# A changed order for the last attention heads, the head norms and the out projection of a two-layer trunk

## The chip, the cores and the metric

The kernel runs on one core of one Trainium2 chip, as one program. The metric is device time in microseconds (us) of an execution, as a median of runs; lower is better. Before the change it is 1693.77 us, the median of 3 runs (1693.08 to 1694.43).

## What is computed

The reference is one step of a two-layer diffusion trunk over 640 tokens of width 1024: 512 latent tokens (tiles 0 to 3 of 128) and 128 context tokens (tile 4). Layer 0 mixes tokens by differential attention, layer 1 by neighbourhood attention on a grid; each is followed by an out projection, a gated residual with layer norm, and a squared-ReLU MLP.

```python
def block(qb):                                   # differential attention, 8 heads
    logits = jnp.einsum('bqhmd,bkhmd->bhmqk', qb, k, preferred_element_type=jnp.float32) * scale
    p = jax.nn.softmax(logits, -1)
    a = p[:, :, 0] - lam * p[:, :, 1]
    return jnp.einsum('bhqk,bkhe->bqhe', a, v).astype(v.dtype)
o = map_query_blocks(block, q)
o = rms_norm(o, subln) * (1.0 - DIFF_LAMBDA_INIT)          # per head: the "head norms"
...
y = attention(x * (1 + scale) + shift) @ w_o                # out projection
x = layer_norm(ALPHA * x + gate * y, ln_g, ln_b)
x = layer_norm(ALPHA * x + gate2 * sq_relu_mlp(x * (1 + scale2) + shift2), ...)
```

Latent tokens read their own keys and the context tokens of a cache; context tokens read context tokens only. All matrix products keep float32 accuracy: every operand is split into a high and a low part (`hhi`/`hlo` for activations, `wh`/`wl` for weights, `aT` high and low for attention weights), and three matmuls (lines 120, 121, 122) make one product.

## The kernel before, in words

TensorE (PE) does the matmuls in an order that is written out by hand: `ORDER0` and `ORDER1` are lists of tokens, and `run` calls the function behind each token in turn. What a token issues to the other engines, VectorE (DVE), ScalarE (ACT), GpSimd (POOL) and the queue of SP, is put in order by the framework's scheduler, and each engine then runs its list strictly in that order.

The tokens of the first layer that matter here, h for a head (0 to 7), b for a tile of queries, t for a tile of tokens, hf for a half of the 1024 output columns:

- `q{h}{t}`, `v{h}{t}`: 24 matmuls of the query/key or the value projection. `r{h}{t}`: PE transposes of rotated queries and keys (line 521); ACT and DVE then write the high and low parts `q` and `K` (lines 523 to 527).
- `S{h}{b}`: scores (lines 461, 462), row maxima on DVE (`mx`, L576), exp on ACT (`E`, L578), difference of the two maps on DVE (L586). `T{h}{b}`: transposes of `E` (L597), then ACT and DVE write `aT` (lines 127, 128). `P{h}`: attention weights times values. `c{h}`, `C{h}`: the same for context queries.
- `Q{h}`: sums of squares of a head's output by matmuls with `mean` (L632); for heads 3, 5, 6, 7 the function `rstd0` (L633 to L652: small DVE steps and one square root on ACT) follows. `D5` (`rn_rows`): a PE transpose, a DVE copy to `rnr` (L659) and a DMA from SP to the DRAM rows `rnd` (L660).
- `N{h}`, the norm of a head. For heads 0 to 5: POOL issues a DMA that broadcasts the row of `rnd` into `X[:, 7, :]` (L727), and one DVE instruction (L728) scales the head's output. There is one such buffer, so the broadcast of one head waits for the scaling of the head before it. For heads 6 and 7 the factor goes through PE (`dg`, L674) and two DVE instructions (L675).
- `m{g}`, `M{g}`: units of the modulation vectors; they also release raw weight buffers `rw`, of which there are three. `X` (`swap`): finishes the modulation, casts heads 0 to 5 to `hhi` on ACT and subtracts on DVE to `hlo`, loads the gates and the residual. These write over the input `h` of the query projections, so they come after the last `q` unit.
- `o{hf}{t}`: the out projection over k tiles 0 to 5 (18 matmuls). `j{hf}{t}`: its k tiles 6 and 7. `g{t}`: gate and residual; `h{t}`: layer norm and transposes; `f{x}`: first units of the MLP.

PSUM has eight banks: four in the pool `M` (512 columns each), and two tiles of two banks for the scores (`S`). A part `o` takes its space in one of three ways. In `before` the way follows from its number x in the list (hf, t): x below `early` (4 in layer 0, 5 in layer 1): a bank of `M`, and `add_gated` (L1084, L1086) at once takes the sum to SBUF, so that `j` starts a fresh bank; the next two: a bank of `M`, held until `g`; the rest: half of a score tile, held until `g`. In layer 0 this gives o00 to o03 early, o04 and o10 held in `M`, o11 to o14 held in a score tile. The second gate tile, which the context tile t = 4 needs, has its broadcast DMA (L735, `gate<-gates`) in a buffer that is free only after the scores S73.

Layer 1 has the same tail with its own letters (`t`, `B`, `Y`, `Z` beside them): `X` there casts heads 0 to 5 and `Y` head 6.

Of the kernel before, what the change touches and what calls it, by code (L numbers as in the profile page):

```python
# [36 lines left out]
EARLY0, EARLY1, PARTS = 4, 5, (10, 9)  # L37
# [4 lines left out]
    e0 e4 A e2 v10 e1 m8 v13 b e3 r00 r04 q10 r02 q14 r01 q12 r03 m9 M8 S00 r10 v11 S01 r11 v12 c0 r14 v14 M9  # L42
    T00 S02 q21 q20 q30 r12 m10 T01 S03 r13 q23 m11 T02 S10 T03 r20 q31 C0 c1 M10 P0 m12 T10 S11 M11 r21 M12
    q22 S12 m13 q24 r22 T11 S13 r23 q32 r24 C1 T12 S20 r30 m14 M13 Q0 T13 M14 c2 P1 S21 T20 r31 q33 S22 T21
    q34 r32 Q1 S23 r33 v21 v20 r34 S30 T23 q40 v24 m15 T22 S32 C2 P2 m16 T30 r40 S31 q42 M16 q41 c3 r42 q43
    q44 T31 S33 r43 v22 r41 v23 M15 C3 r44 Q2 T32 q50 T33 S40 m17 P3 m18 S41 M18 q52 c4 Q3 T40 q51 v33 D3 r51
    r50 q53 M17 S42 v31 r52 q54 T41 S43 r54 r53 v30 S50 T43 v34 T42 v32 S51 q70 q61 C4 P4 c5 m19 T50 q60 m20
    M19 S52 r60 M20 q62 m21 r61 T52 q63 T51 S53 r62 M21 q64 r63 m22 r64 T53 C5 S60 M22 Q4 P5 S61 q71 m23 N2 c6
    Q5 M23 r70 q72 r71 T60 S62 D5 N1 T61 q73 N0 r72 q74 S63 N3 C6 T62 N4 N5 X r73 r74 o00 S70 T63 o02 c7 P6
    o03 T70 S71 Q6 o01 T71 D6 S72 o04 o10 T72 S73 C7 N6 o11 T73 o12 P7 o13 Q7 D7 o14 N7 j00 j10 j01 j11 g0 j12  # L50
    g1 j02 j13 h0 g2 j03 j04 h1 j14 g3 g4 h2 f0 f2 h3 f3 h4 f1
# [1392 lines left out]
```

## Time and profile before

| what | us |
|---|---|
| median of 3 runs | 1693.77 |
| the profiled execution | 1694.21 |
| its span in the trace | 1692.4 |
| PE busy | 1611.3 (95%) |
| DVE busy | 1098.9 (65%) |
| ACT busy | 669.0 (40%) |
| POOL busy | 316.4 (19%) |

The span leaves 1.81 us of the execution outside the trace. PE is the engine that is nearly always busy; 1692.4 - 1611.3 = 81 us of its span are idle. The mean granted clock of TensorE is 0.983 of full speed. Times in the trace are counted from the start of the span: layer 0's tail (from head 5 to the first MLP units) lies at about 300 to 435 us, layer 1's at about 1130 to 1275 us. In a row of the timeline the number in brackets is idle time of that engine before the instruction, with the instruction that ended it.

### The profile page before, as it was taken

To read this page: it belongs to the slowest core of one execution; us is meant where nothing else is said; L and a number is where in the kernel's file an instruction comes from. 1 tells how busy PE (TensorE), PEld (TensorE's weight loads), DVE (VectorE), ACT (ScalarE), POOL (GpSimd) and SP (SyncE) were. 2 spreads that over 40 slices of the span, in tenths; PEclk is the share of its full clock that TensorE was granted. 3 is DMA by queue.
4 is the path that set the end of the run, shared out by engine and by line. 5 is a ranking of instruction groups with operands and counts; after the bars stand their busy time and mean duration, and the time that the engine had idled before them with its cause. 6 is when DMAs were issued, how large, how long until landed. Compare 5 with 4: busy or idle time off the path is not lost. (4 is left out here: it accounts for less than half of the span.)

```text
span 1692.4 us, 23972 instructions
## 1 busy us (share of the span) xinstructions
PE 1611.3 (95%) x9074; PEld 1394.7 (82%) x9074; DVE 1098.9 (65%) x2169; ACT 669.0 (40%) x1366; POOL 316.4 (19%) x260
## 2 busy tenths in 40 slices
...
GB/s 336 130 136 91 102 116 151 103 129 52 124 113 137 199 149 187 162 172 103 75 75 161 126 127 119 148 140 165 14 112 113 63 99 75 76 98 51 100 51 63
DMA packets 61367, 200.62 MB, mean 119 GB/s; under 512 B 7765, under 2 KB 14403, under 8 KB 60227
## 3 DMA queue, kind: packets, MB, share of 16 engines
...
q14 instruction: 45, 0.36, 0.1%
...
## 5 line engine op out<-in xcount | busy, mean ns | idle before, releaser
L195 ACT CAST wh<-rw 128x1024 fp32r<-128x1024 f32 x192 | 200.2, 1053 | 380.1 <-PE M L122 287.9
L197 DVE TENSOR_TENSOR wl<-rw,wh 128x512 fp32r<-128x512 f32 x278 | 216.1, 811 | 128.7 <-ACT wh L195 128.0
L120 PE MATMUL M<-hhi,wh 128*128 128x512 f32 (+2 forms) x768 | 279.0, 363 | 8.1 <-DVE r L1199 7.9
L122 PE MATMUL M<-hhi,wl 128*128 128x512 f32 (+2 forms) x768 | 277.5, 361 | 1.8 <-DVE wl L197 1.8
L121 PE MATMUL M<-hlo,wh 128*128 128x512 f32 (+2 forms) x768 | 277.1, 361 | 0.0
L120 PE MATMUL M<-wh,uhi 128*128 128x512 f32 x640 | 250.9, 392 | 3.1 <-DVE rc L1199 3.1
L120 PE MATMUL M<-wh,hhi 128*128 128x256 f32 (+1 forms) x752 | 244.6, 325 | 8.7 <-DVE tmp L1143 3.2
L122 PE MATMUL M<-wh,ulo 128*128 128x512 f32 x640 | 249.9, 391 | 1.6 <-DVE ulo L128 1.6
L121 PE MATMUL M<-wl,uhi 128*128 128x512 f32 x640 | 249.9, 390 | 0.0
L197 POOL TENSOR_TENSOR wl<-rw,wh 128x512 fp32r<-128x512 f32 x106 | 181.9, 1726 | 345.0 <-ACT wh L195 344.7
L122 PE MATMUL M<-wh,hlo 128*128 128x256 f32 (+1 forms) x752 | 240.1, 319 | 5.0 <-DVE hlo L128 5.0
L121 PE MATMUL M<-wl,hhi 128*128 128x256 f32 (+1 forms) x752 | 239.5, 319 | 0.0
L120 PEld LDWEIGHTS M<-hhi,wh 128*128 128x128 f32 x768 | 146.1, 190 | 26.1 <-issue 8.2
L122 PEld LDWEIGHTS M<-hhi,wl 128*128 128x128 f32 x768 | 145.9, 190 | 20.8 <-DVE wl L197 3.3
L120 PEld LDWEIGHTS M<-wh,hhi 128*128 128x128 f32 x752 | 145.2, 193 | 20.6 <-DVE tmp L1143 3.4
L121 PEld LDWEIGHTS M<-hlo,wh 128*128 128x128 f32 x768 | 146.0, 190 | 17.2
L122 PEld LDWEIGHTS M<-wh,hlo 128*128 128x128 f32 x752 | 144.8, 193 | 17.9 <-DVE hlo L128 9.1
L121 PEld LDWEIGHTS M<-wl,hhi 128*128 128x128 f32 x752 | 145.2, 193 | 8.7
L120 PEld LDWEIGHTS M<-wh,uhi 128*128 128x128 f32 x640 | 120.5, 188 | 28.3 <-issue 3.5
L294 DVE SCALAR_TENSOR_TENSOR jk<-wm,cb 128x1024 bf16<-128x1024 f32 x96 | 141.7, 1476 | 2.9 <-DMA wm<-in_wmodT 1.9
L122 PEld LDWEIGHTS M<-wh,ulo 128*128 128x128 f32 x640 | 120.6, 188 | 27.7 <-DVE ulo L128 2.4
L121 PEld LDWEIGHTS M<-wl,uhi 128*128 128x128 f32 x640 | 120.6, 188 | 25.1 <-DVE wl L197 0.4
(284 smaller groups left out, 2459.9 us busy)
## 6 DMA issues: line engine op xcount, KB each, us to landing
...
```

The costliest lines, as they stand in the source:

```text
L120: te.matmul(out, sh, mh, start=start, stop=False)
L121: te.matmul(out, sh, ml, start=False, stop=False)
L122: te.matmul(out, sl, mh, start=False, stop=stop)
L195: keep(nc.scalar.copy(hi, r))
L197: keep(eng.tensor_tensor(lo[:, k], r[:, k], hi[:, k], ALU.subtract))
L294: op = nc.vector.scalar_tensor_tensor(jk, ws[t], 1.0, cb[:, x, :], ALU.mult, ALU.mult, accum_out=mc[:, t, x : x + 1])
```

## The change

Line numbers of the changed kernel are higher by 2 from line 40 on. Five things change.

1. **The ways of the parts** stand in a table, `PARTS`, with e (early), m (bank of `M`, held) or s (half of a score tile, held) for each. Layer 0 now has o02, o03, o04 and o13 early, o00 and o01 held in `M`, and o10, o11, o12, o14 in a score tile. Layer 1's ways stay as they were.
2. **Layer 0's order after P5.** Before: `S61 q71 m23 N2 c6 Q5 M23 r70 q72 r71 T60 S62 D5 N1 T61 q73 N0 r72 q74 S63 N3 C6 T62 N4 N5 X r73 r74 o00 S70 T63 o02`. After: `q71 S61 r70 q72 r71 N2 q73 Q5 T60 c6 q74 D5 S62 r72 N3 m23 T61 S63 M23 C6 T62 N4 N5 X r73 r74 S70 T63 o02`. So q73 and q74 come ahead, Q5, D5 and m23 later, and S70 T63 stand ahead of the first part.
3. **The parts' order.** Before: `o02 c7 P6 o03 T70 S71 Q6 o01 T71 D6 S72 o04 o10 T72 S73 C7 N6 o11 T73 o12 P7 o13`. After: `o02 c7 P6 o03 T70 S71 Q6 o04 T71 D6 S72 o00 o01 o13 T72 S73 C7 N6 o10 T73 o11 P7 o12`.
4. **Layer 0's end.** g0, g1 and j13 are placed differently among the `j`, and f0 and f2 relative to h2: before `g3 g4 h2 f0 f2`, after `g3 g4 f0 h2 f2`.
5. **Layer 1's order**, one stretch. Before: `P52 c6 q70 B70 S63 t6 T60 S62 q72 X B73 B71 P60 T61 o00 T62 P61`. After: `P52 q70 S63 q72 c6 X B70 t6 T60 S62 B73 B71 P60 o00 T61 T62 P61`.

The tokens N0 to N3 stand earlier in the list (N0 after m20, N1 after r63, N2 after r71, N3 after r72); the scheduler leaves the DVE and POOL instructions of N0 to N3 at the same rows of their engines as before.

```diff
-EARLY0, EARLY1, PARTS = 4, 5, (10, 9)
+PARTS = (
+    "02e 03e 04e 00m 01m 13e 10s 11s 12s 14s",
+    "00e 01e 02e 03e 04e 10m 11m 12s 13s",
+)
...
-    def proj_ops(self, pool, l, late, early, free, ready, tag):
+    def proj_ops(self, pool, l, late, free, ready, tag):
...
-        def slot(x):
-            if x < early + 2:
+        def slot(kind):
+            if kind != "s":
                 return self.M()
...
-        def part(x):
-            hf, t = seq[x]
-            m = slot(x)
-            self.nat(self.h, t, n + hf, m, 0, 512, 0, 6, True, x < early)
-            accs[hf, t] = None if x < early else m
-            if x < early:
+        def part(hf, t, kind):
+            m = slot(kind)
+            self.nat(self.h, t, n + hf, m, 0, 512, 0, 6, True, kind == "e")
+            accs[hf, t] = None if kind == "e" else m
+            if kind == "e":
                 evac = lambda: self.add_gated(late["X"], t, hf, m, late["gate"], True)
...
-        for x, (hf, t) in enumerate(seq):
-            if x < PARTS[l]:
-                op(f"o{hf}{t}", lambda x=x: part(x), "X", *(("Y",) if x >= 2 else ()), *((free,) if x >= early + 2 else ()))
-            op(f"j{hf}{t}", lambda hf=hf, t=t: proj(hf, t), f"o{hf}{t}", *ready)
+        for x, (hf, t, kind) in enumerate(PARTS[l].split()):
+            y = int(hf), int(t), kind
+            op(f"o{hf}{t}", lambda y=y: part(*y), "X", *(("Y",) if x >= 2 else ()), *((free,) if kind == "s" else ()))
+        for hf in range(2):
+            for t in range(NTT):
+                op(f"j{hf}{t}", lambda hf=hf, t=t: proj(hf, t), f"o{hf}{t}", *ready)
```

How the rows move is shown at three places. First PE at the swap of layer 0, in the kernel before, from the last transposes of attention weights ahead of it to the first part (`idf,nt` is r73, `idf,X` is r74, `wh`, `wl` with `hhi`, `hlo` is o00):

```order
L597 MATMUL M_4298<-idf,E_4133 128x128
L320 MATMUL M_4310<-idf,gt_4306 48x128
L521 MATMUL M_4343<-idf,nt_4188 128x128 x3
L521 MATMUL M_4352<-idf,X_549 128x128 x3
L120 MATMUL M_4361<-wh_3396,hhi 128x512
L121 MATMUL M_4361<-wl_3397,hhi 128x512
L122 MATMUL M_4361<-wh_3396,hlo 128x512
```

The same place on PE in the changed kernel (the rows from `K,q` on are S70, those from `idf,E` on are T63, and the last is the first matmul of o02):

```order
L322 MATMUL M_4311<-idf,gt_4307 48x128
L523 MATMUL M_4344<-idf,nt_4076 128x128 x3
L523 MATMUL M_4353<-idf,nt_4188 128x128 x3
L463 MATMUL S_4362<-K_3994,q_546 128x320
L464 MATMUL S_4362<-K_3994,q_546 128x320
L463 MATMUL S_4363<-K_3994,q_546 128x320
...
L599 MATMUL M_4384<-idf,E_4273 128x128 x4
L599 MATMUL M_4391<-idf,E_4273 128x128
L122 MATMUL M_4395<-wh_3396,hhi 128x512
```

The part o00 has left this place; the scores S70 and the transposes T63 follow r74 directly, and the first part is another tile's.

Second, DVE around the copy `rnr` of D5, from which the norms of heads 4 and 5 start. Before:

```order
L576 TENSOR_REDUCE mx_4129<-S_4119 128x1
L576 TENSOR_REDUCE mx_4129<-S_4120 128x1
L659 COPY rnr_4143<-M_4141 10x128
L128 TENSOR_TENSOR aT_4107<-M_4148,aT_4106 128x4x128
L128 TENSOR_TENSOR aT_4107<-M_4155,aT_4106 128x128
```

After (`hlo` is the first of the subtractions of the swap, `wl` a pair of low weight halves):

```order
L130 TENSOR_TENSOR hlo<-X_549,hhi 128x640
L586 RECIPROCAL Z_4124<-Z_4124 128x1
L587 SCALAR_TENSOR_TENSOR c_4125<-Z_4124,zz,neglam 128x1
L578 TENSOR_REDUCE mx_4207<-S_4197 128x1
L588 SCALAR_TENSOR_TENSOR E_4127<-E_4130,c_4125,E_4127 128x128
L578 TENSOR_REDUCE mx_4207<-S_4198 128x1
L199 TENSOR_TENSOR wl_4156<-rw_4147,wh_4155 128x512 x2
L661 COPY rnr_4194<-M_4192 10x128
```

The copy now has one `hlo` and a pair of `wl` ahead of it.

Third, DVE around the scaling of head 5 (N5). Before, where L525 and L527 are the queries and keys of r73 and r74:

```order
L728 SCALAR_TENSOR_TENSOR X_549<-X_549,sub_106 128x640
L128 TENSOR_TENSOR hlo<-X_549,hhi 128x640 x3
L525 SCALAR_TENSOR_TENSOR q_546<-M_4343,q_546 128x2x128
L527 TENSOR_TENSOR K_4051<-M_4343,K_4051 64x128 x2
L525 SCALAR_TENSOR_TENSOR q_546<-M_4352,q_546 128x2x128
L527 TENSOR_TENSOR K_4051<-M_4352,K_4051 64x128 x2
```

After:

```order
L527 SCALAR_TENSOR_TENSOR q_546<-M_4344,q_546 128x2x128
L730 SCALAR_TENSOR_TENSOR X_549<-X_549,sub_106 128x640
L529 TENSOR_TENSOR K_3994<-M_4344,K_3994 64x128 x2
L527 SCALAR_TENSOR_TENSOR q_546<-M_4353,q_546 128x2x128
L130 TENSOR_TENSOR hlo<-X_549,hhi 128x640
L529 TENSOR_TENSOR K_3994<-M_4353,K_3994 64x128 x2
```

The scaling of head 5 and one `hlo` remain ahead of the keys; two `hlo` that followed it have moved to earlier places.

More of the change, by code (lines that the diff above doesn't have):

```diff
@@ L41 @@
 ORDER0 = """
[L42 to L51, printed above, removed]
+    e0 e4 A e2 v10 e1 m8 v13 b e3 r00 r04 q10 r02 q14 r01 q12 r03 m9 M8 S00 r10 v11 S01 r11 v12 c0 r14 v14 M9 T00
@@ L52 @@
+    T51 S53 r62 M21 q64 r63 N1 m22 r64 T53 C5 S60 M22 Q4 P5 q71 S61 r70 q72 r71 N2 q73 Q5 T60 c6 q74 D5 S62 r72 N3
+    m23 T61 S63 M23 C6 T62 N4 N5 X r73 r74 S70 T63 o02 c7 P6 o03 T70 S71 Q6 o04 T71 D6 S72 o00 o01 o13 T72 S73 C7 N6
+    o10 T73 o11 P7 o12 Q7 D7 o14 N7 j00 j10 g0 j01 j11 g1 j12 j02 h0 g2 j03 j04 h1 j13 j14 g3 g4 f0 h2 f2 h3 f3 h4
+    f1
 """
 ORDER1 = """
-    e1 e3 e2 e0 b q03 v04 B00 q00 B03 q01 q02 q12 v11 S00 q10 B01 B02 c0 B10 q11 S01 v13 q13 B12 S02 T00 v12
-    t0 S03 P00 v10 C0 T01 B13 B11 T02 S10 P01 B20 S11 P02 S13 v14 c1 T10 q20 S12 q22 B23 q21 P10 t1 T11 q23 C1
@@ L56 @@
-    T12 P11 S20 B21 q30 S21 q31 c2 T20 P12 B22 q32 S22 q33 S23 t2 B30 q43 v21 P20 T21 v20 S30 q40 C2 B32 T22
-    B31 P21 B33 B40 S31 q41 T30 S33 v23 P22 c3 q42 S32 t3 v24 P30 T31 B42 v22 S40 T32 C3 B41 P31 q50 S41 P32
-    q51 c4 T40 q52 B43 S42 t4 B50 q53 P40 S43 v30 S50 T41 B51 v31 S51 C4 T42 v32 P41 v33 P42 B52 B53 v34 c5
-    T50 q60 P50 S52 q61 S53 t5 q62 B60 T51 q63 B63 S60 B62 B61 C5 T52 P51 q73 S61 q71 P52 c6 q70 B70 S63 t6
-    T60 S62 q72 X B73 B71 P60 T61 o00 T62 P61 C6 S71 P62 o01 Y S70 o02 B72 c7 o03 S72 T70 o04 t7 S73 o10 C7
@@ L61 @@
-    T71 P70 o12 P71 T72 o11 P72 Z o13 j00 j10 j13 g0 j01 j11 j12 g1 j02 h0 g2 j04 j03 g3 h1 j14 g4 h3 h2 f1 f0
-    h4 f3 f2
+    e1 e3 e2 e0 b q03 v04 B00 q00 B03 q01 q02 q12 v11 S00 q10 B01 B02 c0 B10 q11 S01 v13 q13 B12 S02 T00 v12 t0 S03
+    P00 v10 C0 T01 B13 B11 T02 S10 P01 B20 S11 P02 S13 v14 c1 T10 q20 S12 q22 B23 q21 P10 t1 T11 q23 C1 T12 P11 S20
+    B21 q30 S21 q31 c2 T20 P12 B22 q32 S22 q33 S23 t2 B30 q43 v21 P20 T21 v20 S30 q40 C2 B32 T22 B31 P21 B33 B40 S31
+    q41 T30 S33 v23 P22 c3 q42 S32 t3 v24 P30 T31 B42 v22 S40 T32 C3 B41 P31 q50 S41 P32 q51 c4 T40 q52 B43 S42 t4
```

14 lines of the change are left out of this document (11 added, 3 removed).

## Prediction

> **What bounds the kernel now.** I read the page first, then the windows of the two attention tails, then the list of PE's waits, and last the timelines of PE, DVE and POOL at the places that the change touches. The page's first row:
>
> ```profile
> PE 1611.3 (95%) x9074; PEld 1394.7 (82%) x9074; DVE 1098.9 (65%) x2169; ACT 669.0 (40%) x1366; POOL 316.4 (19%) x260
> ```
>
> PE is the bound over the whole run, and the change takes no matmul away and adds none. So it can only move the 1692.4 - 1611.3 = 81 us in which PE stands idle, and time in which it runs at a lower clock. The windows (PE, weight loads, DVE, ACT, POOL busy, then granted clock, DMA share, GB/s) say where these lie:
>
> ```profile
> core 0 of [0], span 1692.4 us
> ...
> 310.00:320.00 10.00, 10.00 (x94) 9.28 (x93) 7.81 (x29) 6.04 (x17) 0.00 (x0) 1.00 0.32 107
> 320.00:330.00 10.00, 9.42 (x75) 8.88 (x74) 9.08 (x29) 8.32 (x19) 0.55 (x1) 1.00 0.10 33
> 330.00:350.00 20.00, 14.79 (x61) 10.89 (x60) 19.07 (x35) 11.69 (x27) 1.07 (x2) 0.74 0.64 222
> 370.00:400.00 30.00, 29.72 (x144) 24.43 (x143) 14.02 (x35) 13.35 (x23) 1.84 (x2) 1.00 0.21 71
> 1140.00:1160.00 20.00, 15.21 (x95) 13.07 (x96) 18.75 (x40) 13.64 (x26) 1.08 (x2) 1.00 0.54 165
> ```
>
> At 330 to 350 (layer 0's swap) and 1140 to 1160 (layer 1's) PE is idle for about 5 us each while DVE is at 95% and 94%: there DVE is the bound. At 370 to 400 it is the other way round, PE at 99%. PE's waits in layer 0's tail, largest first (total, times, longest):
>
> ```profile
> PE M L1060 <- DVE X L1010: 3.5, 2, 3.2
> PE M L521 <- DVE aT L128: 3.0, 1, 3.0
> PE M L120 <- DVE o L675: 2.0, 1, 2.0
> PE M L122 <- DVE hlo L128: 1.7, 2, 1.6
> ```
>
> The second and fourth are the swap: r74, then o00. The first is h2 at the end of the stage, the third is j00 behind N7. PE around r74 and o00:
>
> ```profile
> 335.31 0.90 PE L521 MATMUL M<-idf,X 128*128 128x128 f32 x3 [3.00 <-DVE aT L128]
> 335.86 0.78 PE L120 MATMUL M<-wh,hhi 128*128 128x512 f32 x1
> ...
> 345.59 0.31 PE L461 MATMUL S<-K,q 128*128 128x320 f32 x1
> ...
> 347.23 0.48 PE L120 MATMUL M<-wh,hhi 128*128 128x512 f32 x1
> ```
>
> o00 took from 335.86 to 345.59, 9.7 us. An undisturbed part, o01, takes 4.2 (from 362.12 to 366.33, rows below). Of the 5.5 more, 1.7 are its two waits for `hlo`, and 3.8 are the clock: 0.74 in this window. o02 starts at 347.23, with o00, S70 and T63 done.
>
> **The swap of layer 0: what DVE allows.** The new order does the last two query units earlier, so the casts to `hhi` may start earlier, and puts S70 T63 ahead of the first part. But DVE's work up to the last key of r74 is the same, only rearranged. In before that key is written at 346.4 + 0.3:
>
> ```profile
> L527 DVE TENSOR_TENSOR K<-M,K x4: 284/290/293, 345.0 to 346.4; 64x128 fp32r<-64x128 f32 x4
> ```
>
> From 310 to there DVE is idle for 2.2 + 0.9 + 0.9 us by the windows. With no idle at all the key is there 4 us sooner, at 342.7. S70, T63 and o02 all come after; o02 then starts at 342 to 344; I take 342 as the bound. Against 347.23 this looks like 5 us, but o00 (4.2) is still to come: the gain is at most 1.1 us.
>
> **The swap: what the new order makes of it.** I walk it row by row from P5, up to which both orders are alike. Two chains get longer. The first is the sums of squares:
>
> ```profile
> L633 DVE COPY ssq<-M x1: 165/165/165, 315.8 to 315.8; 128x5 f32<-128x5 f32 x1
> L643 DVE TENSOR_TENSOR ht<-ssq,ht x1: 157/157/157, 316.2 to 316.2; 128x10 f32<-128x10 f32 x1
> L652 DVE TENSOR_TENSOR ssq<-ht,ht x1: 157/157/157, 320.4 to 320.4; 128x10 f32<-128x10 f32 x1
> ```
>
> From the copy of Q5's sums to the last step it takes 4.8 us, ACT's square root in between. A query unit such as q74 takes 3.0, from its first matmul to the next token's:
>
> ```profile
> 326.04 0.36 PE L120 MATMUL M<-wh,hhi 128*128 128x256 f32 x1
> ...
> 329.00 0.30 PE L461 MATMUL S<-K,q 128*128 128x320 f32 x1
> ```
>
> Between Q5 and D5 PE now has only T60, c6 and q74, which I put at 3.6 us together, where it had six tokens; ACT also has the first `hhi` and a weight cast in that queue. I put D5's wait at 2.2 (at least 1.2), and S62 behind it waits 1.3 for its score tile, since the exp of c6 stands behind the same queue. The second chain is D5 to N5:
>
> ```profile
> 324.15 0.27 DVE L659 COPY rnr<-M 10x128 f32<-10x128 f32 x1
> ...
> 341.60 0.88 DVE L728 SCALAR_TENSOR_TENSOR X<-X,sub 128x640 f32<-128x640 f32 x1 [0.77 <-DMA X<-rnd]
> 342.40 2.29 DVE L128 TENSOR_TENSOR hlo<-X,hhi 128x640 fp32r<-128x640 f32 x3
> ```
>
> ```profile
> L727 POOL DMA_DIRECT2D X<-rnd x2: 536/544/553, 326.2 to 337.8; - x2
> ```
>
> The two broadcasts of POOL share a buffer, so that of head 5 went out at 337.8, once head 4 was scaled, and DVE got to head 5 at 341.6. In the new order `rnr` has one `hlo` (0.8) and a pair of `wl` (1.3) ahead of it, its row DMA on SP stands behind four weight loads, whose buffers m23 (now later) must first release, and D5 itself is late. By the walk head 5 is scaled near 346.8, 5 us later. What is queued behind that instruction on DVE: the keys of r73 and r74, for which S70 waits on PE. The stalls of the walk on PE are: D5 2.2, S62 1.3, T61 (its bank waits for the `rnr` copy) 1.8, C6 (its `aTc` stands behind two `wl` pairs) 3.8, the transpose of X 4.5, S70 3.0, together 16.6. Without stalls o02 would start at 347.2 - 5.8 (PE's idle time of 320 to 350 by the windows, 0.6 + 5.2) - 3.8 (clock) - 4.2 (o00) = 333.4; with them at 350.0. Since the waits overlap a little I take 349.4. Net: 349.4 + 4.2 - 347.2 = **+6.4**, between -1.1 (DVE without idle) and +9 (the walk's stalls all a little longer).
>
> For the clock, the row is the o00 above: a pause of 3.0 us was followed by about 9 us of slow matmuls, worth 3.8. Some of the new pauses are as long, so up to 4 us more stand in the range, none in the sum, since half the slow time would fall into waits. The Trainium skill, "TensorE: Matmul & The Clock Gate", Part 1, has the clock halved after an idle window of about 3.4 us; here 3.0 was enough. By its figure only the two longest pauses would count, and the sum would be the same.
>
> **T72 to N6 in layer 0.** Here three of the four banks of `M` are taken at once in the new order: o00 and o01 are held, and o04, though early, can't be emptied before the second gate tile is there.
>
> ```profile
> 378.77 0.59 POOL L735 DMA_DIRECT2D gate<-gates  x1 [7.42 <-PE S L462]
> ```
>
> That DMA waits for S73, the last reader of the buffer. Before, only o04 and o10 are held there. What one bank alone costs is read from a part and the transposes after it:
>
> ```profile
> 362.12 0.48 PE L120 MATMUL M<-wh,hhi 128*128 128x512 f32 x1
> ...
> 366.33 0.71 PE L597 MATMUL M<-idf,E 128*128 128x128 f32 x5
> ```
>
> ```profile
> L127 ACT CAST aT<-M x2: 272/429/586, 367.0 to 367.4; 128x512 fp32r<-128x512 f32 x1, 128x128 fp32r<-128x128 f32 x1
> L128 DVE TENSOR_TENSOR aT<-M,aT x2: 282/482/683, 367.9 to 368.6; 128x512 fp32r<-128x512 f32 x1, 128x128 fp32r<-128x128 f32 x1
> ```
>
> Transposes that start at 366.33 leave their bank only when DVE has subtracted, 367.9 + 0.7 = 368.6, 2.3 us later. With one free bank T72 waits for o13's gating (1.5) and between its two tiles (1.3), and N6's two matmuls wait for the `o` copy (1.5) and for DVE (0.9): 5.2, where PE now loses 0.2. **+5.0**, between 0 (the gate's DMA comes in time for one more bank) and +6.5. DVE is half idle here (14 of 30 us), so nothing else hides it; PE has no spare work, its order is fixed.
>
> **The ends.** o00 is held, so j00 adds to its own bank and its k tile 6 needn't wait for N7: **-0.5** of the 2.0. f0 ahead of h2 gives PE work in h2's wait of 3.2, but the same DVE chain of gates, norms and `hlo` ends the stage: **-1.0**, between 0 and -1.7. N0 to N3 move nothing on DVE or POOL: 0.
>
> **Layer 1.** PE's waits at 1136 to 1160, and the six `hlo` there:
>
> ```profile
> PE M L122 <- DVE hlo L128: 3.3, 2, 1.7
> PE M L860 <- issue: 1.1, 1, 1.1
> PE S L461 <- DVE mn L840: 0.8, 1, 0.8
> ```
>
> ```profile
> L128 DVE TENSOR_TENSOR hlo<-X,hhi x6: 817/819/826, 1149.3 to 1154.8; 128x640 fp32r<-128x640 f32 x6
> ```
>
> PE loses 5.2 us, and o00 ends with the last `hlo`. The new order takes c6 and t6 behind X: the casts and subtractions of X come ahead of c6's exp and division on ACT and DVE, so t6 now waits, by some 3.5, and o00 no longer does. DVE's sum is unchanged. **-1.5**, between -4.3 and +2.
>
> **The sum.** 6.4 + 5.0 - 0.5 - 1.0 - 1.5 = +8.4. The profiled execution is 1694.21 (span 1692.4 and 1.81 outside); it becomes 1702.6. It lies 0.44 above the median of the runs, so on the median's scale 1702.2, given as **1702**. The case's own range runs from 1697 to 1708.
>
> **Rivals.**
> *The cover works (faster).* S70 and T63 fill the wait that o00 had, DVE runs without idle, and no pause is long enough for the clock. The point that decides is the scaling of head 5: it must start near 338 instead of the walk's 346.8. For it: q74 has m23, M23, D5 and S62 behind it instead of ahead, and the `hhi` casts that wait for it can follow. Against it: DVE is 95% busy in that window already. Then the swap gives -1.1, T72 to N6 +0.5, the ends -2.2 and layer 1 -4.3: -7.1, 1686.7.
> *Cancelled (no change).* The row DMA of D5 isn't held up by the weight loads, so head 5 is scaled near 342: swap +1.5; o04's gate comes early enough that T72 loses only 1.5; ends and layer 1 give 3.0 back: 0, 1694.
> *The clock falls too (slower still).* Short waits between groups of matmuls at T72 to N6 and after X bring the clock down as at o00: 3.8 per part for two parts, +7.6 on the forecast: 1710. For it: the window at 330 to 350. Against it: that pause was 3.0, those at T72 are 1.5 and less. The Trainium skill, "TensorE: Matmul & The Clock Gate", "A second HAM failure mode", says that a kernel cycling through PSUM banks with short idles loses clock in just this way; no window of before with pauses under 2 us alone shows it.
>
> **How the numbers follow.** Forecast 0.50, cover 0.20, cancelled 0.15, clock 0.15. The measurement can tell about 0.2% here, 3.4 us. Faster by more than that is the cover, 0.20; within it the cancelled case, 0.15; slower the other two, 0.65. The forecast's own 1697 to 1708, the cancelled case and most of each outer one give 1687 to 1710.
>
> **What would show it.** Right, in the trace of the changed kernel: head 5's scaling (L730) later than 341.6, PE waits at L659, at the transposes after C6 and at S70, o02 at 349 or later; waits of 1 us or more at T72 and at N6; no wait for `hlo` at layer 1's o00, but one at t6. Wrong: o02 starting by 344, PE at 99% around T72, or layer 1's stretch shorter by over 4 us.

## The result and the profile after

The changed kernel takes **1722.82 us**, the median of 4 runs (1721.19 to 1723.57), against 1694.10 (1693.08 to 1694.43, 4 runs) before: ratio **1.0177**, 95% interval 1.0164 to 1.0189. The ratio on record lies a little above the 1.0170 that these two medians give. It is slower by 28.7 us, where 8 were forecast; the direction was right, the size lies outside the range.

The page of the changed kernel, span and busy times:

```profile
span 1719.4 us, 23969 instructions
...
PE 1619.4 (94%) x9074; PEld 1404.2 (82%) x9074; DVE 1101.8 (64%) x2169; ACT 670.9 (39%) x1366; POOL 315.4 (18%) x260
```

The same 9074 matmuls keep PE busy 1619.4 - 1611.3 = 8.1 us longer, which is time at a lower clock. PE's idle time grows from 81.1 to 1719.4 - 1619.4 = 100.0, by 18.9. Together these are the 27.0 us of the two spans.

Where they lie is read from PE's timelines, by the first and the last matmul of a token (us):

| stage | before | after | more |
|---|---|---|---|
| layer 0, end of P5 to the start of o02 | 38.15 | 44.04 | 5.9 |
| o00: before in the row above, now behind S72 | | 4.1 | 4.1 |
| start of o02 to the end of N7, without o00 | 55.8 | 63.1 | 7.3 |
| *end of P5 to the end of N7, the three rows together* | 93.92 | 111.25 | 17.3 |
| end of N7 to the end of f1 | 40.61 | 44.26 | 3.65 |
| layer 1, end of S61 to the end of P61 | 28.56 | 34.52 | 6.0 |
| end of P61 to the end of o13 | 45.30 | 47.29 | 2.0 |

The stages give 28.9; all the rest of this execution was 1.9 shorter. Two cautions for the experiments: the rest of the kernel varies by 2 to 4 us between executions, and the stage from N7 to f1 by 3.5 (41.9 to 45.4 in kernels that are alike there). The stretch from P5 to T63 took 38.4, 38.4 and 40.1 in three kernels that are alike up to there (the kernel before, the ends alone and the mended parts), so differences under 2 us there tell little.

**Layer 0's swap.** PE's timeline of the changed kernel, the rows with waits and the start of o02 (start, us, engine, line, operation; idle time before it in brackets):

```profile
325.22 0.27 PE L659 MATMUL M<-idf,ssq 128*10 128x128 f32 x1 [1.95 <-DVE ssq L654]
327.01 0.63 PE L463 MATMUL S<-K,q 128*128 128x320 f32 x1 [1.22 <-ACT E L580]
...
338.66 0.33 PE L122 MATMUL M<-aTc,V 128*128 128x128 f32 x1 [4.31 <-ACT aTc L129]
...
340.02 0.47 PE L123 MATMUL M<-aTc,V 128*128 128x128 f32 x1 [1.04 <-DVE aTc L130]
...
345.76 0.38 PE L322 MATMUL M<-idf,gt 128*48 128x128 f32 x1 [3.96 <-DVE gt L317]
...
349.83 0.60 PE L463 MATMUL S<-K,q 128*128 128x320 f32 x1 [1.34 <-DVE K L529]
...
351.95 0.78 PE L122 MATMUL M<-wh,hhi 128*128 128x512 f32 x1
```

The waits are those of the walk: D5, S62, the two at C6, X, S70, together 13.8. The windows of the same stretch (PE, weight loads, DVE, ACT, POOL busy, granted clock, DMA share, GB/s):

```profile
320.00:330.00 10.00, 6.82 (x48) 5.78 (x50) 7.13 (x21) 9.31 (x18) 0.00 (x0) 0.80 0.17 59
330.00:340.00 10.00, 4.68 (x33) 3.26 (x25) 7.38 (x18) 5.55 (x13) 0.55 (x1) 0.84 0.59 210
340.00:350.00 10.00, 4.67 (x19) 3.93 (x20) 8.97 (x20) 5.09 (x13) 1.07 (x2) 0.50 0.38 120
```

Before, the clock was 1.00 up to 330 and 0.74 from there to 350. Now it is below 1 in all three windows. The second long chain is the norm of heads 4 and 5; DVE's rows, then SP's, then POOL's:

```profile
331.42 0.27 DVE L661 COPY rnr<-M 10x128 f32<-10x128 f32 x1
...
343.85 0.89 DVE L730 SCALAR_TENSOR_TENSOR X<-X,sub 128x640 f32<-128x640 f32 x1 [0.17 <-DMA X<-rnd]
...
348.48 0.88 DVE L730 SCALAR_TENSOR_TENSOR X<-X,sub 128x640 f32<-128x640 f32 x1 [0.56 <-DMA X<-rnd]
349.40 0.28 DVE L529 TENSOR_TENSOR K<-M,K 64x128 fp32r<-64x128 f32 x1
```

```profile
330.69 1.66 SPq L185 DMA_DIRECT2D rw<-in_w  x3
332.44 0.32 SPq L662 DMA_DIRECT2D rnd<-rnr  x1
```

```profile
339.43 0.55 POOL L729 DMA_DIRECT2D X<-rnd  x1 [41.92 <-DMA rnd<-rnr]
```

The row of D5 goes out at 332.44, right behind three weight loads, and POOL's broadcast that waits for it follows at 339.43, 7.0 later. Before, `rnr` was there at 324.15 and the broadcast went out at 326.2. Head 5 is scaled at 348.48, and the key that S70 waits for comes right behind it.

**T72 to N6 and o10.** PE's rows, then the clock in three windows:

```profile
387.46 0.66 PE L599 MATMUL M<-idf,E 128*128 128x128 f32 x4 [1.51 <-DVE X L1088]
389.52 0.33 PE L599 MATMUL M<-idf,E 128*128 128x128 f32 x1 [1.40 <-DVE aT L130]
...
392.81 1.10 PE L676 MATMUL M<-dg,ones 128*128 128x512 f32 x2 [1.51 <-ACT o L624]
394.75 0.80 PE L676 MATMUL M<-dg,ones 128*128 128x128 f32 x2 [0.84 <-DVE o L677]
395.20 0.77 PE L122 MATMUL S<-wh,hhi 128*128 128x512 f32 x1
...
400.56 0.71 PE L599 MATMUL M<-idf,E 128*128 128x128 f32 x5
```

```profile
392.00:394.00 2.00, 1.10 (x2) 0.30 (x2) 0.95 (x5) 1.45 (x5) 0.16 (x1) 1.00 0.52 178
394.00:396.00 2.00, 1.25 (x4) 1.16 (x5) 2.00 (x3) 0.00 (x0) 0.00 (x0) 0.57 0.24 84
396.00:398.00 2.00, 2.00 (x6) 1.57 (x6) 1.80 (x4) 0.72 (x1) 0.00 (x0) 0.58 0.00 0
```

The four waits that the prediction priced at 5.2 are 5.3. Behind them the clock falls, and o10 takes 400.56 - 395.20 = 5.4 where an undisturbed part takes 4.2.

**Layer 1.** One wait on PE makes the loss, t6's for the probabilities of c6. PE's row, then DVE's and ACT's rows ahead of it:

```profile
1171.66 0.66 PE L914 MATMUL M<-idf,Ec 128*128 128x128 f32 x2 [9.43 <-DVE Ec L909]
```

```profile
1163.17 2.49 DVE L199 TENSOR_TENSOR wl<-rw,wh 128x512 fp32r<-128x512 f32 x4
1165.69 0.86 DVE L817 TENSOR_TENSOR K<-M,K 64x256 fp32r<-64x256 f32 x2
1166.58 0.42 DVE L905 TENSOR_REDUCE mn<-S 128x2 f32<-128x256 f32 x1
...
1171.09 0.42 DVE L909 TENSOR_TENSOR Ec<-Ec,Z 128x256 f32<-128x256 f32 x1
```

```profile
1163.94 2.60 ACT L129 CAST hhi<-X 128x640 fp32r<-128x640 f32 x4
...
1168.32 0.37 ACT L907 ACTIVATE Ec<-S,mn 128x128 f32<-128x128 f32 x1
```

PE has written c6's scores by 1162.2 (1171.66 - 9.43). Their maximum waits on DVE behind four `wl` and two keys (1166.58), their exp on ACT behind the casts of X (1168.32), their division on DVE behind `hlo` and `wl` (1171.09). Each of three steps stands in a block of X's work. Of the 6.0 in the table, 4.8 are idle time (waits of 0.82, 1.06, 1.70 and 1.57 before, of 9.43 and 0.53 after); the other 1.2 are matmuls that took longer.

### The profile page after: what moved, and what is told of

Same layout as the page of the kernel before. It is cut to its first block, busy times and chain, and to the rows that moved or that the text cites. A ratio compares the mean times of both kernels' runs of the same rounds, so it can differ in the third digit from the quotient of the medians.

```text
span 1719.4 us, 23969 instructions
## 1 busy us (share of the span) xinstructions
PE 1619.4 (94%) x9074; PEld 1404.2 (82%) x9074; DVE 1101.8 (64%) x2169; ACT 670.9 (39%) x1366; POOL 315.4 (18%) x260
## 5 line engine op out<-in xcount | busy, mean ns | idle before, releaser
L123 PEld LDWEIGHTS M<-hlo,wh 128*128 128x128 f32 x768 | 146.3, 190 | 17.3
```

What stands on the lines that cost most here:

```text
L123: te.matmul(out, sh, ml, start=False, stop=False)
```

## The experiments

The theory after this reading: at both swaps DVE and ACT have a block of work that each engine does strictly in its order, and whatever on PE needs a fresh result from behind the block waits for all of it. Only a part such as o00, which takes `hlo` piece by piece, can use that time, and both reorderings put something else there. The rivals: the weight units m23, the late row of D5, the early q73 and q74, or the clock, each as a cost of its own. Some kernels start from the changed kernel and undo a part; the others start from the kernel before and do a part alone. Each is given by its own runs, beside runs of the kernel before on the same chip (medians 1692.3 to 1694.3).

**Layer 1's order alone undone** (from the changed kernel):

```diff
-P52 q70 S63 q72 c6 X B70 t6 T60 S62 B73 B71 P60 o00 T61 T62 P61
+P52 c6 q70 B70 S63 t6 T60 S62 q72 X B73 B71 P60 T61 o00 T62 P61
```

> Layer 1's order of before, everything else as changed. Theory A (the loss of layer 1 is its own stretch: t6 waits 9.43 us in the changed kernel): the stretch from P52 to P61 goes from 29.9 back to about 24.0 us and the time falls by 6 to 8, to 1715 to 1717. Rival (the loss there is an after-effect of layer 0, a shifted clock or late weights): under 2 us gained, about 1721 to 1723.

Measured 1717.37, ratio 1.0135 (1.0116 to 1.0153): 5.5 less than the changed kernel, and S61 to P61 takes 28.54 again, as before the change. The 2.0 between P61 and o13 are gone as well (45.5, before 45.3). Layer 1's part of the loss comes from this stretch of the order alone.

**c6 ahead of the swap in layer 1** (from the changed kernel):

```diff
-P52 q70 S63 q72 c6 X B70 t6 T60
+P52 c6 q70 S63 q72 X B70 t6 T60
```

> Only c6 of layer 1 moves back ahead of q70, so that its maximum and exp no longer stand behind the casts and subtractions of X; q72 and o00 stay as changed. Theory A (t6's 9.43 us is c6's chain in the queues of ACT and DVE): the wait at t6 falls under 1 us, the time by 6 to 10, to 1713 to 1717; if q72 ahead is of use it is below the run with the whole order of before. Rival (DVE is the bound there, whatever stands first): the wait moves to o00's hlo or T60 and at most 3 us are gained, 1720 to 1723.

Measured 1723.36, ratio 1.0162 (1.0134 to 1.0189): no gain. t6's wait is gone, but PE's timeline has it again at P60:

```profile
1173.93 0.58 PE L869 MATMUL O<-PT,V 128*128 128x256 f32 x1 [5.59 <-ACT PT L129]
1177.93 0.58 PE L870 MATMUL O<-PT,V 128*128 128x256 f32 x1 [3.42 <-DVE PT L130]
```

5.59 + 3.42 = 9.0. So c6's place alone does not make the wait: the next token that needs a cast or a subtraction from behind X's block inherits it.

**o00 as the first consumer behind X in layer 1** (from the changed kernel, c6 early as well):

```diff
-P52 q70 S63 q72 c6 X B70 t6 T60 S62 B73 B71 P60 o00 T61 T62 P61
+P52 c6 q70 S63 q72 X B70 t6 T60 S62 o00 B73 B71 P60 T61 T62 P61
```

> Layer 1 with c6 early and o00 ahead of P60 (T60, S62, o00, P60, T61), the rest as changed. With c6 early alone the wait went from t6 to P60, whose weights stand behind X's casts and subtractions on ACT and DVE. Theory A in its second form (behind X only o00 can use DVE's block piece by piece; any work that needs a fresh DVE result waits for the whole block): the 9 us at P60 shrink to under 5, the stretch from S61 to P61 falls from 34.5 or 35.3 to 29 to 31, the time to 1716 to 1719. Rival (DVE's sum sets the end whatever stands first): within 1.5 of the changed kernel.

Measured 1714.14, ratio 1.0130 (1.0114 to 1.0145), and the stage takes 30.98 instead of 34.52. PE's row with the wait that is left:

```profile
1163.42 0.76 PE L122 MATMUL M<-wh,hhi 128*128 128x512 f32 x1 [4.38 <-DVE K L817]
```

With o00 in the gap half of the wait is used. It is still 2.4 above before, where q72 and X came later.

**m23 early in layer 0** (from the changed kernel):

```diff
-P5 q71 S61 r70 q72 r71 N2 q73 Q5 T60 c6 q74 D5 S62 r72 N3 m23 T61 S63 M23 C6
+P5 q71 S61 m23 r70 q72 M23 r71 N2 q73 Q5 T60 c6 q74 D5 S62 r72 N3 T61 S63 C6
```

> Layer 0's m23 and M23 move back ahead of r70 and r71, the rest as changed. Theory B (late m23 holds two raw weight buffers, the late loads delay the low weight halves ahead of C6's operand and stand ahead of D5's row DMA): the 4.3 us wait at C6 goes, the row's way from SP to POOL falls from 7.0 to under 3 us, head 5 is scaled 4 or more us sooner, the time falls by 4 to 7, to 1716 to 1719. Rival (D5 behind q74 and the square root alone set the end): less than 1.5 gained, 1721.5 or more.

Measured 1714.21, ratio 1.0126 (1.0102 to 1.0151). PE's rows at the swap:

```profile
337.17 0.63 PE L462 MATMUL S<-K,q 128*128 128x320 f32 x1 [3.07 <-ACT E L579]
...
340.19 0.47 PE L122 MATMUL M<-aTc,V 128*128 128x128 f32 x1 [0.17 <-DVE aTc L129]
...
348.01 0.60 PE L462 MATMUL S<-K,q 128*128 128x320 f32 x1 [4.16 <-DVE K L528]
```

C6's wait is gone (0.2 instead of 5.4): it came from weight loads that had to wait for the buffers of m23. In the changed kernel ACT's weight cast at 337.40, right ahead of the cast that C6 reads, waited 2.0 for such a load. But S63 now waits 3.1 and S70 4.2. P5 to T63 becomes 3.7 shorter (40.66 against 44.39), and the rest of the loss stays. The time falls by 8.6, more than this stretch gives; another 2.0 lie between N7 and f1, within that stage's spread. Head 5 comes no sooner (40.3 after P5, in the changed kernel 40.6), though the theory had the norms earlier.

**Q5 and D5 early too** (from the changed kernel):

```diff
-P5 q71 S61 r70 q72 r71 N2 q73 Q5 T60 c6 q74 D5 S62 r72 N3 m23 T61 S63 M23 C6
+P5 q71 S61 m23 Q5 r70 q72 M23 r71 N2 q73 D5 T60 c6 q74 S62 r72 N3 T61 S63 C6
```

> The changed order with m23 behind S61, Q5 behind m23, M23 behind q72 and D5 ahead of T60 and q74; q73 and q74 stay early. Theory B in its finer form (the chains from Q5 and from m23 are too late, the early query units do no harm): D5 doesn't wait, the row goes out 5 us or more sooner, head 5 is scaled by 342 instead of 348.5, the stretch from P5 to T63 falls to 37 to 39 us, below the run with m23 alone (40.7); the time 1713 to 1716. Rival (late raw weights alone): as the run with m23 alone.

Measured 1721.77, ratio 1.0166 (1.0142 to 1.0189). I expected more than from m23 alone and got none: D5's wait went, and waits at q73 (1.5), S62 (2.0), S63 (3.3), C6 (1.3) and S70 (5.0) stand in its place. The first row is POOL's broadcast for head 4, the second DVE's scaling of it:

```profile
328.87 0.56 POOL L728 DMA_DIRECT2D X<-rnd  x1 [27.85 <-DVE mx L577]
```

```profile
343.49 0.88 DVE L729 SCALAR_TENSOR_TENSOR X<-X,sub 128x640 f32<-128x640 f32 x1
```

The broadcast is 10.6 earlier than in the changed kernel (339.43), the scaling just 0.4 (343.85), and head 5 comes at 348.38 as there (348.48). DVE has no idle time before it: it stands behind maxima, keys and weight halves on DVE's list. An early row alone does not bring the norms forward; their place on DVE was late as well.

**The query stretch of before, in the changed kernel:**

```diff
-P5 q71 S61 r70 q72 r71 N2 q73 Q5 T60 c6 q74 D5 S62 r72 N3 m23 T61 S63 M23 C6 T62 N4 N5 X r73 r74 S70 T63 o02
+P5 S61 q71 m23 N2 c6 Q5 M23 r70 q72 r71 T60 S62 D5 T61 q73 r72 q74 S63 N3 C6 T62 N4 N5 X r73 r74 S70 T63 o02
```

> Layer 0's order from P5 to C6 as before (q73, q74, Q5, D5, m23 at their old places), the rest as changed, S70 and T63 still ahead of o02. Theory B (the moved query units, Q5, D5 and m23 make the loss at the swap, not the place of o00): the stretch from P5 to the end of T63 falls from 44.4 to about 38 us, the time to 1715 to 1718. Rival (without o00 beside the hlo of the swap PE idles there in any order): 42 us or more, under 2.5 gained.

Measured 1720.45, ratio 1.0166 (1.0151 to 1.0181): hardly less than the changed kernel, where I had expected 1715 to 1718. The stretch from P5 to T63 takes 39.4, without o00. PE's row of S70:

```profile
345.91 0.60 PE L462 MATMUL S<-K,q 128*128 128x320 f32 x1 [8.10 <-DVE K L528]
```

S70 waits 8.1 us just where o00 stood. So o00 stood in a wait of PE that S70 and T63 can't use; whether another token could is not shown.

**The three parts of layer 0's change, each alone in the kernel before.** First the query stretch, with o00 left where it was:

```diff
-P5 S61 q71 m23 N2 c6 Q5 M23 r70 q72 r71 T60 S62 D5 N1 T61 q73 N0 r72 q74 S63 N3 C6 T62
+P5 q71 S61 r70 q72 r71 N2 q73 Q5 T60 c6 q74 D5 S62 r72 N3 m23 T61 S63 M23 C6 T62
```

> The kernel before with the changed order from P5 to r74 alone (early q73, q74; late Q5, D5, m23); parts, ends and layer 1 as before. Theory B (late chains of D5 and of the raw weights cost time, but o00 stands beside the swap's subtractions again and takes part of the wait): 1696 to 1700. Rival 1 (the earlier casts of hhi pay once o00 follows r74): 1688 to 1692. Rival 2 (what the changed kernel lost at its swap is all this stretch's doing, 6 us and the clock): 1702 or more.

Measured 1701.71, ratio 1.0053 (1.0033 to 1.0073): 9.4 slower, between the theory (up to 1700) and the second rival (1702 or more). SP's and POOL's rows are as in the changed kernel, a row behind three weight loads (332.14, then 333.64), the broadcast at 339.48, head 5 scaled at 349.61.

Second the parts, with o00 out of its place (`PARTS` and their order of the changed kernel, S70 T63 directly behind r74):

```diff
-    "00e 01e 02e 03e 04m 10m 11s 12s 13s 14s",
+    "02e 03e 04e 00m 01m 13e 10s 11s 12s 14s",
...
-r73 r74 o00 S70 T63 o02 c7 P6 o03 T70 S71 Q6 o01 T71 D6 S72 o04 o10 T72 S73 C7 N6 o11 T73 o12 P7 o13 Q7 D7 o14
+r73 r74 S70 T63 o02 c7 P6 o03 T70 S71 Q6 o04 T71 D6 S72 o00 o01 o13 T72 S73 C7 N6 o10 T73 o11 P7 o12 Q7 D7 o14
```

> The kernel before with the new ways and order of the parts alone (S70, T63 ahead of o02; o00, o01 held, o04 early, o13 early); query stretch, ends and layer 1 as before. Theory E (S70 needs keys that DVE writes behind all subtractions of the swap, so nothing but o00 can use that wait; and three banks are held at T72): swap 4 to 5 worse, T72 to o10 6 to 8 worse, together 1703 to 1708. Rival (parts only matter with the new query stretch): 1697 or less.

Measured 1714.44, ratio 1.0118 (1.0090 to 1.0145): 22 slower, more than expected. PE's row of S70, then DVE's of g0:

```profile
347.38 0.60 PE L462 MATMUL S<-K,q 128*128 128x320 f32 x1 [7.97 <-DVE K L528]
```

```profile
430.71 0.69 DVE L1142 TENSOR_TENSOR tmp<-S,gate 128x512 f32<-128x512 f32 x1 [3.20 <-PE S L123]
```

P5 to T63 takes 39.14, no less than the 38.39 of before, though o00 is no longer in it; o00 then costs its whole length later, T72 and N6 wait 2.9 and 1.9, and N7 to f1 takes 45.84 where before has 40.61. The spans differ by 1714.1 - 1692.4 = 21.7, of which PE is busy 8.2 longer (1619.5), so idle 13.5. The 3.2 of the second row is a new wait, taken up below.

Third the order of the ends:

```diff
-N7 j00 j10 j01 j11 g0 j12 g1 j02 j13 h0 g2 j03 j04 h1 j14 g3 g4 h2 f0 f2 h3 f3 h4 f1
+N7 j00 j10 g0 j01 j11 g1 j12 j02 h0 g2 j03 j04 h1 j13 j14 g3 g4 f0 h2 f2 h3 f3 h4 f1
```

> The kernel before with the new order of j, g, h and f at layer 0's end alone. Theory (that order is near neutral; DVE's chain ends the stage either way): within 1.5 of before, 1692 to 1695. Rival (it costs the 3.7 us of the stretch from N7 to the last MLP unit): 1696 to 1698.

Measured 1692.62 (10 runs), ratio 0.9998 (0.9986 to 1.0010): no difference. The same undone in the changed kernel:

```diff
-N7 j00 j10 g0 j01 j11 g1 j12 j02 h0 g2 j03 j04 h1 j13 j14 g3 g4 f0 h2 f2 h3 f3 h4 f1
+N7 j00 j10 j01 j11 g0 j12 g1 j02 j13 h0 g2 j03 j04 h1 j14 g3 g4 h2 f0 f2 h3 f3 h4 f1
```

> Only the order of j, g, h and f at layer 0's end as before. Theory D (that order costs the 3.7 us by which the stretch from N7 to the last MLP unit grew): the stretch falls from 44.3 to 41 or less, the time by 2.5 to 4, to 1719 to 1720. Rival (the stretch grew by what reaches it, late weights and clock, and would in any order): under 1 gained.

Measured 1722.97, ratio 1.0182 (1.0163 to 1.0200): the time of the changed kernel. So the order of the ends is not what makes the stage longer there.

Query stretch 9.4, parts 22, ends 0, layer 1 5.5: the sum of about 37 is more than the 28.7, because the first two overlap. P5 to N7 is 8.2 longer with the stretch alone and 16.0 with the parts alone, but 17.3 with both, so 6.9 of the overlap lie there: S70's wait of 8.0 is down to 1.3 once PE has lost its time earlier.

**What of the query stretch costs.** Three kernels from the kernel before. Only q73 and q74 early:

```diff
-r70 q72 r71 T60 S62 D5 N1 T61 q73 N0 r72 q74 S63 N3 C6
+r70 q72 r71 q73 T60 q74 S62 D5 N1 T61 N0 r72 S63 N3 C6
```

> The kernel before with only q73 and q74 moved ahead of T60 and of S62; m23, Q5 and D5 keep their order among the rest. Theory B2 (the early units put casts to hhi and their subtractions ahead of D5's copy and of the exp on ACT and DVE, which delays heads 4 and 5): the stretch grows by 3 to 6, 1695 to 1699. Rival (the early units are harmless, and o00 waits less for hlo): 1 to 3 gained, 1689 to 1692.

Only m23 late:

```diff
-P5 S61 q71 m23 N2 c6 Q5 M23 r70 q72 r71 T60 S62 D5 N1 T61 q73 N0 r72 q74 S63 N3 C6
+P5 S61 q71 N2 c6 Q5 r70 q72 r71 T60 S62 D5 N1 T61 q73 N0 r72 m23 q74 S63 M23 N3 C6
```

> The kernel before with m23 placed behind r72 and M23 behind S63, as late as the changed order has them; all else as before. Theory B1 (late m23 holds the raw weight buffers, the weights of the out projection arrive late, their halves and the modulation's end stand late on DVE): the stretch from P5 to T63 grows from 38.4 by 4 or more, 1696 to 1701. Rival (only together with the late D5 does it cost anything): within 1.5 of before.

Both together:

```diff
-P5 S61 q71 m23 N2 c6 Q5 M23 r70 q72 r71 T60 S62 D5 N1 T61 q73 N0 r72 q74 S63 N3 C6
+P5 S61 q71 N2 c6 Q5 r70 q72 r71 q73 T60 q74 S62 D5 N1 T61 N0 r72 m23 S63 M23 N3 C6
```

> The kernel before with q73, q74 early and m23, M23 late together, Q5 and D5 in their old order among the rest. Each alone left the time as it was. Theory B3 (the row of heads 4 and 5 has slack of some 7 us between its broadcast and the scaling; each edit uses part of it, both together more than there is): the stretch from P5 to T63 grows from 38.4 to 43 or more, 1697 to 1702. Rival (Q5 behind q73, which only the whole stretch has, is what costs): within 2.5 of before.

Measured 1693.10 (ratio 0.9995, 0.9985 to 1.0006), 1694.42 (1.0003, 0.9993 to 1.0014) and 1693.55 (1.0010, 0.9996 to 1.0024), each of 10 runs: no loss is seen, against the theory in all three expectations. By the intervals at most 1.0, 2.4 and 4.1 us are lost. In the profiled executions P5 to N7 is 1.3, 1.8 and 2.2 longer than before, about as much as that stretch varies. Waits of 5.4, 6.5 and 5.6 do appear on PE in these kernels, but they take the place of those at r74 and in o00. SP's and POOL's rows of the third kernel show that the norms have time to spare there:

```profile
326.21 0.30 SPq L661 DMA_DIRECT2D rnd<-rnr  x1
326.94 8.39 SPq L184 DMA_DIRECT2D rw<-in_w  x5
```

```profile
328.00 0.55 POOL L728 DMA_DIRECT2D X<-rnd  x1 [30.89 <-DMA rnd<-rnr]
```

The row goes ahead of the weight loads and is followed by the broadcast within 1.8, and head 4 is scaled at 337.93, ten us later: there is slack. D5 stands behind q74 here too, though ahead of S62. What this kernel lacks of the whole stretch is Q5 behind q73, c6 behind T60 (both are ahead of r70 here) and S61 behind q71. With the whole stretch the broadcast comes at 339.48 and head 4 waits 1.7 for it, so the slack is gone. By what is left over, these places make most of the 9.4, the late Q5 being the likeliest. It is not shown to act through the late row alone, since in the changed kernel an early row brought nothing; moving only Q5, or only c6 and S61, in the kernel before was not tried, and this stays open.

**What of the parts costs.** o00 back behind r74, and o04 held beside o01 instead of emptied early (from the kernel with the parts alone):

```diff
-    "02e 03e 04e 00m 01m 13e 10s 11s 12s 14s",
+    "00e 02e 03e 01m 04m 13e 10s 11s 12s 14s",
...
-r73 r74 S70 T63 o02 c7 P6 o03 T70 S71 Q6 o04 T71 D6 S72 o00 o01 o13 T72
+r73 r74 o00 S70 T63 o02 c7 P6 o03 T70 S71 Q6 T71 D6 S72 o01 o04 o13 T72
```

> The kernel before with the new parts' order except that o00 is early again and stands behind r74, ahead of S70, and o01 and o04 are the held ones (o13 stays early, o10 with o11 and o12 with o14 share score tiles). Theory E (the parts' 16 us from P5 to N7 are o00's missing at the swap and the third held bank): the stretch from P5 to N7 returns to 93 to 97 us, against 109.9 with the new parts alone; the time within 6 of before, what is left lying behind N7. Rival (the early o13 or the new pairs in the score tiles matter ahead of N7 too): 99 or more.

Measured 1704.90, ratio 1.0057 (1.0040 to 1.0074): 9.5 of the 22 come back, P5 to N7 is 102.0. I had expected 93 to 97. PE's timeline has a new wait, since no part is left between S71 and T71:

```profile
367.47 0.74 PE L598 MATMUL M<-idf,E 128*128 128x128 f32 x5 [3.47 <-ACT ht L647]
```

In the changed kernel, the same choice of tiles without moving any token's place (o00 where o04 was, o01 and o04 held):

```diff
-    "02e 03e 04e 00m 01m 13e 10s 11s 12s 14s",
+    "02e 03e 00e 01m 04m 13e 10s 11s 12s 14s",
...
-Q6 o04 T71 D6 S72 o00 o01 o13 T72
+Q6 o00 T71 D6 S72 o01 o04 o13 T72
```

> Layer 0 with o00 early in o04's place and o01, o04 held instead of o00, o01: two banks held at T72 instead of three, as before the change; the rest as changed. Theory C (the waits at T72 and N6 are bank shortage from o04, whose gate comes after S73): 2.9 and 2.35 us of waits and some 2.5 us of slow clock at T72, N6 and o10 go, the time falls by 5 to 8, to 1715 to 1718. Rival (ACT and DVE are late there for another reason): 1 us or less gained.

Measured 1713.98, ratio 1.0120 (1.0104 to 1.0136), 8.8 less than the changed kernel. PE's rows, where the changed kernel has four waits of 5.3 together:

```profile
387.17 0.33 PE L598 MATMUL M<-idf,E 128*128 128x128 f32 x1 [1.08 <-DVE X L1087]
...
390.38 0.49 PE L675 MATMUL M<-dg,ones 128*128 128x128 f32 x2 [0.51 <-ACT o L623]
```

P5 to N7 is 5.7 shorter and o10 takes 4.4. Here o01 and o04 hold a bank of `M` and o00 no longer does. So a third held bank was one too many, as the prediction had it. o04 holds one either way until the second gate tile is there, whose DMA POOL issues at 391.6 in the changed kernel and at 389.2 here.

Last, the 3.2 that g0 waits in the kernel with the parts alone. There o10 and o11 share a score tile; here o12 takes o11's place:

```diff
-N6 o10 T73 o11 P7 o12 Q7
+N6 o10 T73 o12 P7 o11 Q7
```

> As the run with the new parts alone, but o12 ahead of o11, so that o10 and o12 share one score tile and o11 and o14 the other. Theory G (g0 reads o10's half of a tile into which j11 writes ahead of it, DVE waits 3.2 us there and its chain ends the stage that much later): DVE's wait of 3.2 us goes, the stretch from N7 to the last MLP unit falls from 45.8 to 41.5 to 43.5, the time by 2 to 4 against 1714. Rival (the stretch is long from clock and late weights): 45 or more.

Measured 1711.10, ratio 1.0112 (1.0094 to 1.0130), and N7 to f1 falls from 45.84 to 42.00. The intervals of the two times overlap, and 42.00 lies within the spread of this stage; what tells is DVE's row of g0:

```profile
427.27 0.69 DVE L1142 TENSOR_TENSOR tmp<-S,gate 128x512 f32<-128x512 f32 x1 [0.41 <-PE S L123]
```

g0 reads o10's half of the tile while j11 writes into the other half, and waits for that. The wait was for the neighbour's matmuls, not for its own; what makes DVE wait for them is not shown.

**The clock by itself.** In the kernel before, 26 needless transposes ahead of r73, into columns that r73's own transposes then overwrite, so that PE isn't idle before r74:

```diff
+            for _ in range(26 if (i, t) == (7, 3) else 0):
+                nc.tensor.transpose(tp[:, :P], flat[:, :P], self.idf)
```

> The kernel before with 26 needless transposes into r73's own bank ahead of its three, so that PE is busy in the 3.0 us in which it waited for r74's bank; nothing else moves. Theory F (the clock lost after that pause costs 3.8 us of its own): o00's matmuls run at full clock and the time falls by 2.5 to 4, to 1690 to 1691. Rival (o00 ends with the last subtraction of the swap whatever the clock, and DVE sets that): within 1 us of before, o02 starting at the same time.

Measured 1691.26 (10 runs), ratio 0.9990 (0.9980 to 1.0000). By the ratio that is 1.7 us back, by its interval 0 to 3.4, so a gain is not shown; o00's slow clock was priced at 3.8. Nor is it seen at its place: o02 starts 40.1 after P5, before 38.2, and in the mended parts, alike up to there, 39.8. PE's rows, then the windows:

```profile
331.07 3.06 PE L521 MATMUL M<-idf,nt 128*128 128x128 f32 x26 [0.47 <-ACT o L624]
...
337.94 0.80 PE L122 MATMUL M<-wh,hlo 128*128 128x512 f32 x1 [2.32 <-DVE hlo L128]
```

```profile
334.00:336.00 2.00, 1.47 (x10) 0.79 (x7) 2.00 (x5) 2.00 (x4) 0.00 (x0) 1.00 0.88 324
336.00:338.00 2.00, 0.06 (x1) 0.06 (x1) 2.00 (x6) 1.92 (x7) 0.54 (x1) 0.81 0.85 225
338.00:340.00 2.00, 2.00 (x4) 1.28 (x5) 2.00 (x3) 0.00 (x0) 0.00 (x0) 0.50 0.82 288
```

The pause of 3.0 is filled, but o00 comes sooner to DVE's `hlo`, waits 2.3 there, and the clock falls after all. So o00 ends no sooner, and its faster start is given back in the wait for `hlo`. What o00 would cost at full clock throughout the run doesn't tell. The Trainium skill, "TensorE: Matmul & The Clock Gate", Part 4, says that transposes don't count as activity for the clock in the way of other matmuls. This run can't test that: the pause of 2.3 may be enough by itself. In the kernel before, j00 waits 2.04 behind N7, with ordinary matmuls ahead of it, and the clock falls to 0.51:

```profile
406.00:408.00 2.00, 1.96 (x6) 1.40 (x6) 1.07 (x2) 0.01 (x1) 0.00 (x0) 0.51 0.90 334
```

Such a fall is not certain. The same wait of 2.04 at j00 left the clock at 1.00 in six other kernels, this one among them (1.00 from 406 to 408 in the kernel with q73 and q74 early).

## Why the prediction was right and wrong, by its steps

**What bounds, and that PE can only lose idle time and clock: right.** Both show in the page, 18.9 and 8.1.

**The swap of layer 0, +6.4: the mechanism right, the size too small; 5.9 + 4.1 = +10.0 measured.** D5 2.2 forecast, 1.95 measured; S62 1.3 and 1.22; C6 3.8 and 5.35; X 4.5 and 3.96; S70 3.0 and 1.34; only T61's 1.8 did not come. The sum of the waits is even smaller than forecast (13.8 against 16.6). The step that failed is the clock: "up to 4 us more stand in the range, none in the sum, since half the slow time would fall into waits". The kernel before had a second case that the prediction did not price, j00's pause of 2.04 with 0.51 behind it, so a pause can cost clock without being as long as 3.0. Without waits o02 would start 24.3 after P5 (333.4 - 309.1 by the prediction's figures); with 13.8 it would be 38.1, and it is 44.0: 5.9 of slower matmuls. Head 5 came at 348.48, 40.6 after P5, where the walk had 37.7. The row's 7.0 behind three weight loads are part of that chain, but in the kernel with Q5 and D5 early an earlier row brought nothing back. That o00's place was worth more than its 4.2 us, the prediction saw only as bound ("o00 is still to come"); the two kernels in which S70 waits 8 us there show that S70 and T63 can't fill that time.

**T72 to N6, +5.0: the waits right within 0.1 (5.3, of which 0.2 was there before), the cause shown** by the kernel that holds o04. What was missing is again the clock: 7.3 - 5.1 = 2.2 more from o02 to N7, o10 among it. The prediction held against this that the pauses are "1.5 and less"; that argument failed, since the clock fell to 0.57 behind pauses of which none was longer than 1.51. The rule that stood beside it, "A second HAM failure mode" of the Trainium skill's "TensorE: Matmul & The Clock Gate", agrees with this trace. In nine other kernels with waits at these four places (0.84 to 1.52) the clock is 0.50 to 0.70 behind them, so this loss is steady. The rival that the clock falls too priced this at +7.6; the busy time has +8.1.

**The ends, -1.5: wrong, +3.65 in the profiled execution.** j00 did not start sooner: it waits 2.4 for `hhi`, where it waited 2.0. The order of the ends was worth nothing, alone or undone. The step that failed is "f0 ahead of h2 gives PE work in h2's wait of 3.2": that wait did shrink, to 1.5, but the next token f2 waits in its place, for the score tile that g4 reads:

```profile
450.50 0.58 PE L122 MATMUL S<-hhi,wh 128*128 128x256 f32 x1 [3.57 <-DVE tmp L1143]
```

Before, f2 waited 1.1. All waits of the stage are 8.8, before 6.6. f2 starts 31.3 after the end of N7, before 30.0, which is 1.4 of the 3.65; the other 2.3 come behind f2, where the clock is 0.52 from 450 to 456. In the kernel with o00 first in layer 1, alike in this stage, f2 also starts 31.3 after N7, but there the clock stays at 1.00 from 450 to 456 behind the same wait (3.56), and f1 ends 10.6 after f2's start, as in the kernel before, and not 12.9. So those 2.3 come and go with the clock between executions. The term also looked only at the tokens whose order the diff changes there. The table of parts decides which two parts share a score tile, and with the parts alone g0 waits 3.2 on DVE while its neighbour is being written and the stage takes 45.84. In the changed kernel itself g0 stands ahead of j11 and has no such wait; with the order of the ends undone there, g0 waits 2.7 behind j11 again and the stage takes 45.7.

**Layer 1, -1.5: wrong, +6.0 and 2.0 more behind it.** The failed step: "so t6 now waits, by some 3.5, and o00 no longer does". The first half had the right token and the wrong length, 9.43; the second half came true. The walk let c6 pass X's block once; its maximum, exp and division are three steps on two engines in turn, and each stands behind a piece of the block. This is the largest single miss. Undoing the stretch takes back 5.5 of the time.

**N0 to N3 move nothing: right.**

**The rivals.** The cover failed at its own deciding point, head 5 near 338. The clock rival had its mechanism right at T72 and behind X, but was priced without the misses at the ends and in layer 1. By stages the forecast of 8.4 misses 3.6 in the swap, 2.3 at T72 to N6, 5.2 at the ends and 9.5 in layer 1: 20.6 of the 28.9.
